# The first half of an adaLN modulation: sums moved to TensorE, and the first tile of x loaded ahead of the shift columns

## The chip, the core and the metric

The kernel runs on one core of a Trainium2 chip. The metric is device time in microseconds (us). Five engines matter: TensorE (PE in the rows, PEld its weight loads), VectorE (DVE), ScalarE (ACT), GpSimd (POOL), and SyncE (SP), which issues the transfers.

## What is computed

One layer of a decoder trunk over a sequence of 2048 tokens with 1024 columns, in float32. What the change touches is its first line:

```python
c_act = jax.nn.silu(c)                                        # 1024 values
shift, scale, gate = jnp.split(c_act @ w_ada + b_ada, 3, axis=-1)
h = rms_norm(x, norm_g) * (1 + scale[:, None]) + shift[:, None]
proj = h @ w_in                                               # 4232 columns
```

The projection feeds three mixers (a gated MLP, an mLSTM and a stick-breaking attention); their outputs go through one output projection, are multiplied by the gate and added to x.

## The kernel before

The 2048 tokens are 16 tiles of 128, taken in blocks of 5, 5 and 6 tiles. The first block is the prologue of this text. For its five tiles, x is loaded (`load_x`), ScalarE squares and sums it and GpSimd makes the scale of each row (`rms_x`), VectorE multiplies it by that scale and by `hscale`, VectorE or GpSimd adds `hshift` (`mod_x`: VectorE for tiles 0, 2 and 4, GpSimd for 1 and 3), TensorE transposes it, and ScalarE and VectorE write it as a high and a low part into `hT` (`hT_half`). Then TensorE multiplies it with the weights, which are split into two parts as well (`weights`), in three matmuls per 128 rows of weights (`proj_tc`, lines 297 to 299).

All of that is done in two halves of 512 columns: first columns 0 to 511 of all five tiles with the first half of the modulation, and the first four of eight row groups of the weights; then the other half. Of each half of the modulation, `ada` makes `hscale` (from the scale columns of w_ada) and `hshift` (from the shift columns). It sums over the 1024 rows of w_ada in eight groups of 128: six by VectorE, one multiply-add each into `acc`, which starts as a row of b_ada over zeros; two by TensorE into PSUM; and one matmul with a matrix of ones adds up `acc` over the partitions. So the sums stand in every partition. A float32 matmul is two instructions in the trace.

The transfers of w_ada come in four parts of 1 MiB for each half, scale columns first. All loads and stores of the rows below stand in one queue, SP's, in the order of the program. The tiles `x4va` and `x4gu` are the two halves of tile 4; `wad` is w_ada, `st` the staged weights, `wr` the split ones, `pada` the PSUM of the modulation, `pt` that of the transposes, `pc` that of the projection. The memory of `wad` and of the staged weights is used again for later loads, which wait until it is free. Two of the staged buffers exist, so the third set of weights needs the first to be split.

The order of the instructions on each engine is not the order of the code: a scheduler orders them with a modelled timeline, so an edit near the start can move instructions later too.

Of the kernel before, what the change touches and what calls it, by code (L numbers as in the profile page):

```python
# [18 lines left out]
P = 128  # L19
# [3 lines left out]
KT = D // P  # L23
# [10 lines left out]
def hybrid_block_kernel(ctx: ExitStack, tc: tile.TileContext, x, c, norm_g, w_ada, b_ada, w_in,  # L34
                        ga_v_norm, ga_ws, ga_bs, mb_conv_w, mb_conv_b, mb_b_i, mb_b_f, mb_h_norm,
                        sc_q_norm, sc_k_norm, w_out, out):
    nc = tc.nc
# [33 lines left out]
    c_act = const.tile([P, KT], F32, name="c_act")  # L71
# [36 lines left out]
    def flat(t):  # L108
        return t.rearrange("p a t -> p (a t)")

    def t512(name):
        return flat(tmp.tile([P, 4, P], F32, tag="t512", bufs=T5, name=name))
# [3 lines left out]
    def load_x(i, j, halves=None):  # L116
        if halves is None:
            if j % 4 < 2:
                xt = tmp.tile([P, D], F32, tag="xt", name=f"xt{i}")
            else:  # L120
                xt = stk.tile([P, D], F32, tag="aT", bufs=4, name=f"xt{i}")
            nc.sync.dma_start(xt, x[0, i * P:(i + 1) * P, :])
            xtiles[i] = [[xt], None]
        else:
            for hh in range(2):
                nc.sync.dma_start(halves[hh], x[0, i * P:(i + 1) * P, hh * 512:(hh + 1) * 512])
            xtiles[i] = [halves, None]

    def rms_x(i):
        parts = xtiles[i][0]  # L130
        ssq = tmp.tile([P, 2], F32, tag="ssq", bufs=6, name=f"ssq{i}")
        for n, xp in enumerate(parts):
            junk = tmp.tile([P, D], BF16, tag="t512", bufs=T5, name=f"junk{i}_{n}")
            nc.scalar.activation(junk[:, :xp.shape[1]], xp, AF.Square, accum_out=ssq[:, n:n + 1])
        s0 = ssq[:, 0:1]
        if len(parts) == 2:
            nc.gpsimd.tensor_tensor(s0, s0, ssq[:, 1:2], ALU.add)
        nc.gpsimd.tensor_scalar(s0, s0, 1.0 / D, EPS, ALU.mult, ALU.add)
        nc.gpsimd.tensor_tensor(s0, s0, neghalf[:, 0:1], ALU.pow)
        xtiles[i][1] = s0  # L140
# [11 lines left out]
    def vg_halves(i):  # L152
        return [tmp.tile([P, 2 * NBMAX * 64], F32, tag=tag, bufs=1, name=f"x{i}{tag}")[:, 0:512] for tag in ("va", "gu")]
# [11 lines left out]
    def load_w(src, segs, kp):  # L165
        st = stg_p.tile([P, 2, WMAX], F32, tag="st", name=f"st{ntag[0]}_{kp}")
        o = 0
        for c0, w in segs:
            nc.sync.dma_start(st[:, :, o:o + w],
                              src[kp * 256:(kp + 1) * 256, c0:c0 + w].rearrange("(a p) f -> p a f", p=P))  # L170
            o += w
        return st

    def weights(src, segs, kps=range(KT // 2), staged=None):

        W = sum(w for _, w in segs)
        tiles = []
        key = segs[0][0]
        made = split.setdefault(key, {})
        for kp in kps:  # L180
            if kp * 2 in made:
                for k in (2 * kp, 2 * kp + 1):
                    wt = wr_p.tile([P, 2, WMAX], F32R, tag="wr", name=f"wr{ntag[0]}_{k}")
                    nc.sync.dma_start(wt[:, :, :W].bitcast(F32), made[k])
                    tiles.append(wt)
                continue
            st = staged[kp] if staged else load_w(src, segs, kp)
            for a in range(2):
                wt = wr_p.tile([P, 2, WMAX], F32R, tag="wr", name=f"wr{ntag[0]}_{kp}_{a}")
                nc.scalar.copy(wt[:, 0, :W], st[:, a, :W])  # L190
                (nc.vector if a == 0 else nc.gpsimd).tensor_tensor(  # L191
                    wt[:, 1, :W], st[:, a, :W], wt[:, 0, :W].bitcast(F32), ALU.subtract)
                made[2 * kp + a] = dram.tile([P, 2, W], F32, name=f"w_d{key}_{2 * kp + a}")
                nc.sync.dma_start(made[2 * kp + a], wt[:, :, :W].bitcast(F32))
                tiles.append(wt)
        ntag[0] += 1
        return tiles

    def c_segs(p):
        segs = [(OFF["cq"] + p * P, P), (OFF["ck"] + p * P, P), (OFF["cv"] + p * P, P)]  # L200
        return segs + [(OFF["bi"], 8)] if p == 0 else segs
# [10 lines left out]
        nc.gpsimd.memset(brow[n], 0.0)  # L212
    g_bc = [stk.tile([P, 512], F32, tag="be", bufs=4, name=f"g_bc{n}") for n in range(2)]

    def ada_load(half):
        for n, c0 in enumerate((1024 + 512 * half, 512 * half)):
            for hh in range(2):
                nc.sync.dma_start(wad_buf[2 * n + hh], w_ada[0, 512 * hh:512 * hh + 512, c0:c0 + 512]
                                  .rearrange("(k p) f -> p k f", p=P))

    def ada(half):
        cs = slice(half * 512, half * 512 + 512)
        for n, c0 in enumerate((1024 + 512 * half, 512 * half)):
            pa = flat(pat.tile([P, 4, P], F32, tag="at", name=f"pada{half}_{n}"))
            acc = brow[c0 // 512]
            w0, w1 = wad_buf[2 * n], wad_buf[2 * n + 1]
            for k in range(6):
                nc.vector.scalar_tensor_tensor(acc, (w0 if k < 4 else w1)[:, k % 4, :], c_act[:, k:k + 1], acc,
                                               ALU.mult, ALU.add)
            for k in (6, 7):  # L230
                nc.tensor.matmul(pa, lhsT=c_act[:, k:k + 1].to_broadcast([P, P]), rhs=w1[:, k % 4, :],
                                 start=k == 6, stop=False)
            nc.tensor.matmul(pa, lhsT=ones_sq, rhs=acc, start=False, stop=True)
            if n == 0:
                nc.vector.scalar_tensor_tensor(hscale[:, cs], pa, 1.0, g_bc[half], ALU.add, ALU.mult)
            else:
                nc.scalar.copy(hshift[:, cs], pa)

    nc.sync.dma_start(crow, c.rearrange("o (k p) -> (o k) p", p=P))
    for n in (2, 0, 3, 1):  # L240
        nc.sync.dma_start(brow[n][0:1, :], b_ada[:, n * 512:(n + 1) * 512])
    ada_load(0)
    for n in range(2):
        nc.sync.dma_start(g_bc[n], norm_g[:, n * 512:(n + 1) * 512].broadcast_to([P, 512]))
    nc.gpsimd.dma_start(rows[R_CW:R_CW + 24, :], mb_conv_w.rearrange("o t (m p) -> (o t m) p", p=P))
    nc.gpsimd.dma_start(rows[R_CB:R_CB + 6, :], mb_conv_b.rearrange("o (m p) -> (o m) p", p=P))
    nc.gpsimd.dma_start(rows[R_BS:R_BS + 4, :], ga_bs.rearrange("o g p -> (o g) p"))
# [9 lines left out]

    NB0 = BLOCKS[0]
    staged = {}
    for j in range(NB0):  # L260
        halves = None
        if j == 4:
            halves = vg_halves(4)
        elif j == 5:
            halves = [t512(f"x5_{hh}") for hh in range(2)]
        load_x(j, j, halves)
        if j < 2:
            staged[j] = load_w(w_in[0], c_segs(0), j)
    ada(0)
    for j in range(NB0):  # L270
        rms_x(j)
        if j == 0:
            wt0 = weights(w_in[0], c_segs(0), range(0, 2), staged)
    ada_load(1)
    pr = pat.tile([P, 4, P], F32, tag="at", name="pr")
    nc.tensor.transpose(pr[:, 0, 0:36], rows, ident[0:36, 0:36])
# [524 lines left out]
    for j in range(NB0):  # L801
# [8 lines left out]
        ps0.append(ps)  # L810
        run(proj_tc(ps[:, :W0], wt0, j, W0, range(0, 4)))
    ada(1)
    wt0 += weights(w_in[0], c_segs(0), range(2, 4), staged)
    nc.sync.dma_start(vn_bc, ga_v_norm.rearrange("o g d -> o (g d)").broadcast_to([P, 256]))
# [24 lines left out]
    for b, nb in enumerate(BLOCKS):  # L839
# [30 lines left out]
        else:  # L870
# [4 lines left out]
            for m, _ in enumerate(chain(tail, islice(cp, lead * KT + 1))):  # L875
                j = m // KT - 1
# [205 lines left out]
```

## Time and profile before

| | |
|---|---|
| median of 3 runs | 1470.33 us (1470.11 to 1472.72) |
| the profiled execution, own time | 1471.23 us |
| its span, first to last instruction | 1469.2 us |
| TensorE busy | 1393.4 us (95%) |
| TensorE weight loads busy | 1298.2 us (88%) |
| VectorE busy | 1018.8 us (69%) |
| ScalarE busy | 676.5 us (46%) |
| GpSimd busy | 647.6 us (44%) |
| mean rate of the transfers | 159 GB/s, above 290 in the first twentieth of the span |

Busy time says how long an engine had an instruction under way. A matmul on TensorE can be pipelined, so a busy TensorE is not one at its peak: its clock has two levels, 1.2 and 2.4 GHz, which the profile shows as a granted clock of 0.5 and 1.0. The profile was taken from a single execution; its durations are those of that execution.

### The profile page before, as it was taken

Reading aid. Unit: us, or ns where it says so; the run is one execution under the profiler, and the core shown is the slowest. Engines: PE = TensorE matmul, PEld = TensorE weight load, DVE = VectorE, ACT = ScalarE, POOL = GpSimd, SP = SyncE. Lnnn points to the kernel's source line nnn. Section 1 sums busy time; section 2 is a strip of 40 time slices with the busy share of each in tenths; the row PEclk is TensorE's granted clock in tenths of the full one; section 3 lists DMA queues with packets and bytes.
Section 4 is the critical chain, followed back from the end, with each engine's and each line's share of the span. In section 5 each row is a group of like instructions: output and inputs, shape, how many; then the busy total and the mean of one; then the engine's idle time right before and its main releaser. Section 6 shows DMA issues by size and latency. Waiting matters only on the chain.

```text
span 1469.2 us, 24957 instructions
## 1 busy us (share of the span) xinstructions
PE 1393.4 (95%) x8468; PEld 1298.2 (88%) x8468; DVE 1018.8 (69%) x1778; ACT 676.5 (46%) x1656; POOL 647.6 (44%) x1140
## 2 busy tenths in 40 slices
PE   5999999898999999999999999999999978999998
PEld 3789999798999999988999899989999867888887
DVE  6797554676995666588799976778778788444543
ACT  3364454453554444346467655556455655111110
POOL 4473553743433432554343343434445337435442
PEclk8999999999999999999999999999999999999999
DMA  9866776666535533633433344303432435555541
GB/s 324 293 204 206 237 228 197 208 202 236 191 128 176 198 116 124 222 100 127 148 105 126 104 146 137 102 15 120 157 102 69 156 113 153 178 160 154 175 154 58
DMA packets 187103, 233.19 MB, mean 159 GB/s; under 512 B 22714, under 2 KB 160344, under 8 KB 186976
## 3 DMA queue, kind: packets, MB, share of 16 engines
q1 hardware_dynamic: 186752, 231.59, 48.5%
q8 instruction: 67, 1.10, 0.3%
q14 instruction: 60, 0.49, 0.1%
q0 software_dynamic: 224, 0.02, 0.0%
HBM read 159.24 MB, written 72.31 MB: 158 GB/s over the span
## 4 chain that ended last, share of the span: by engine, by line
PE 66%; DVE 15%; DMA 6%; issue 5%; POOL 4%; ACT 2%; SPq 1%; POOLq 0%; DVEq 0%; ACTq 0%
DVE bb L414 5%; PE av L444 5%; PE at L429 4%; PE pc L297 4%; PE pc L299 4%; PE pc L298 4%; PE po L995 4%; PE po L997 3%; PE po L996 3%; PE pg L297 3%; PE pg L298 3%; PE pg L299 3%; DMA st<-in_w_in_dram 2%; PE z L401 2%; PE z L402 2%
## 5 line engine op out<-in xcount | busy, mean ns | idle before, releaser
L414 DVE TENSOR_TENSOR_SCAN bb<-bb,bb 128x513 f32<-128x513 f32 x144 | 191.3, 1328 | 25.5 <-ACT bb L406 24.7
L418 POOL TENSOR_TENSOR be<-be,bb 128x512 f32<-128x512 f32 (+3 forms) x120 | 133.0, 1108 | 132.9 <-DVE bb L414 81.4
L432 DVE TENSOR_TENSOR aT<-at,aT 128x512 fp32r<-128x512 f32 (+3 forms) x240 | 142.3, 598 | 39.8 <-ACT aT L431 39.1
L406 ACT ACTIVATE bb<-z 128x512 f32<-128x512 f32 (+3 forms) x240 | 130.2, 543 | 80.5 <-PE z L402 61.2
L444 PE MATMUL av<-aT,Vst 128*128 128x256 f32 x816 | 148.7, 295 | 17.8 <-DVE aT L432 13.0
L431 ACT CAST aT<-at 128x512 fp32r<-128x512 f32 (+3 forms) x240 | 126.6, 529 | 83.8 <-PE at L429 82.7
L444 PEld LDWEIGHTS av<-aT,Vst 128*128 128x128 f32 x816 | 119.9, 189 | 30.1 <-DVE aT L432 21.0
L429 PE MATMUL at<-ident,be 128*128 128x128 f32 x816 | 132.7, 274 | 5.2 <-DVE aT L432 2.3
L297 PE MATMUL pc<-wr,hT 128*128 128x384 f32 (+1 forms) x384 | 134.8, 355 | 2.8 <-ACT hT L290 1.3
L299 PE MATMUL pc<-wr,hT 128*128 128x384 f32 (+1 forms) x384 | 134.7, 351 | 1.6 <-DVE hT L291 1.5
L298 PE MATMUL pc<-wr,hT 128*128 128x384 f32 (+1 forms) x384 | 133.4, 347 | 0.0
L407 ACT ACTIVATE be<-z 128x512 f32<-128x512 f32 (+3 forms) x240 | 131.7, 549 | 0.0
L429 PEld LDWEIGHTS at<-ident,be 128*128 128x128 f32 x816 | 99.2, 141 | 14.2 <-DVE aT L432 3.7
L995 PE MATMUL po<-wo,yT 128*128 128x512 f32 x256 | 104.9, 410 | 0.3 <-ACT yT L984 0.3
L414 DVE TENSOR_TENSOR_SCAN bb<-bb 128x129 f32<-128x129 f32 (+3 forms) x96 | 87.1, 911 | 23.3 <-POOL bb L409 16.8
L405 POOL MEMSET bb<- 128x1 f32 x240 | 23.5, 100 | 177.6 <-DVE bb L414 123.6
L996 PE MATMUL po<-wo,yT 128*128 128x512 f32 x256 | 101.6, 397 | 0.0
L997 PE MATMUL po<-wo,yT 128*128 128x512 f32 x256 | 101.4, 399 | 0.0
L487 PE MATMUL pb<-hT,wr 128*128 128x320 f32 (+1 forms) x288 | 93.2, 324 | 1.2 <-DMA wr<-w_d 1.2
L489 PE MATMUL pb<-hT,wr 128*128 128x320 f32 (+1 forms) x288 | 92.1, 323 | 1.8 <-DVE wr L191 1.3
L297 PE MATMUL pa<-wr,hT 128*128 128x384 f32 x256 | 88.2, 347 | 5.1 <-DVE qk L360 2.4
L401 PE MATMUL z<-Kst,Qst 128*128 128x512 f32 (+3 forms) x240 | 90.2, 385 | 2.4 <-DVE Kst L371 1.6
(273 smaller groups left out, 3900.3 us busy)
## 6 DMA issues: line engine op xcount, KB each, us to landing
wr<-w_d SPq DMA_DIRECT2D x160, 384.0 KB, 5.6
w_d<-wr SPq DMA_DIRECT2D x80, 384.0 KB, 3.4
wad<-in_w_ada_dram SPq DMA_DIRECT2D x8, 1024.0 KB, 6.7
xo<-in_x_dram SPq DMA_DIRECT2D x16, 512.0 KB, 3.8
out_dram<-o SPq DMA_DIRECT2D x31, 256.0 KB, 2.9
xt<-in_x_dram SPq DMA_DIRECT2D x15, 512.0 KB, 4.9
st<-in_w_in_dram SPq DMA_DIRECT2D x60, 128.0 KB, 3.4
wr<-w_d SPq DMA_DIRECT2D x16, 392.0 KB, 6.2
```

The costliest lines, as they stand in the source:

```text
L297: nc.tensor.matmul(ps, lhsT=hT[:, 0, k, cols], rhs=wt[k][:, 0, :W], start=k == 0, stop=False)
L298: nc.tensor.matmul(ps, lhsT=hT[:, 0, k, cols], rhs=wt[k][:, 1, :W], start=False, stop=False)
L299: nc.tensor.matmul(ps, lhsT=hT[:, 1, k, cols], rhs=wt[k][:, 0, :W], start=False, stop=k == KT - 1)
L407: nc.scalar.activation(be[:, :w], z[:, :w], AF.Sigmoid)
L414: nc.vector.tensor_tensor_scan(rev, rev, rev, carry.get((i, h), 1.0), ALU.mult, ALU.bypass)
L418: eng.tensor_tensor(be[:, :w], be[:, :w], bb[:, 1:w + 1], ALU.mult)
L429: nc.tensor.transpose(at[:, s, :], be[:, s * P:(s + 1) * P], ident)
L432: nc.vector.tensor_tensor(aT[:, :nb_, 1, :], at[:, :nb_, :], aT[:, :nb_, 0, :].bitcast(F32), ALU.subtract)
L444: nc.tensor.matmul(flat(av), lhsT=Vst[:, s0 + s, h, :], rhs=flat(aT[:, s]), start=(s0 + s == i), stop=(s0 + s == 0))
L995: nc.tensor.matmul(po, lhsT=yT[:, 0, k, :], rhs=wo[k][:, 0, cs], start=k == 0, stop=False)
L996: nc.tensor.matmul(po, lhsT=yT[:, 0, k, :], rhs=wo[k][:, 1, cs], start=False, stop=False)
L997: nc.tensor.matmul(po, lhsT=yT[:, 1, k, :], rhs=wo[k][:, 0, cs], start=False, stop=k == KT - 1)
```

## The change

Two edits. In the first half of the modulation all eight groups of rows are summed by TensorE (`nv = 0`), so VectorE's twelve multiply-adds of that half go and twelve matmuls come; the second half stays as it was. And the loads are put in another order: the scale columns of w_ada, x tile 0, the first half of norm_g, then the shift columns; the second half of norm_g goes behind all x tiles. The squares of tile 0 are written ahead of the others.

```diff
-    def ada_load(half):
-        for n, c0 in enumerate((1024 + 512 * half, 512 * half)):
+    def ada_load(half, ns=range(2)):
+        for n in ns:
+            c0 = 512 * half + (1024 if n == 0 else 0)
...
-            for k in range(6):
+            nv = 6 if half else 0
+            for k in range(nv):
                 nc.vector.scalar_tensor_tensor(acc, (w0 if k < 4 else w1)[:, k % 4, :], c_act[:, k:k + 1], acc,
                                                ALU.mult, ALU.add)
-            for k in (6, 7):
-                nc.tensor.matmul(pa, lhsT=c_act[:, k:k + 1].to_broadcast([P, P]), rhs=w1[:, k % 4, :],
-                                 start=k == 6, stop=False)
+            for k in range(nv, KT):
+                nc.tensor.matmul(pa, lhsT=c_act[:, k:k + 1].to_broadcast([P, P]), rhs=(w0 if k < 4 else w1)[:, k % 4, :],
+                                 start=k == nv, stop=False)
             nc.tensor.matmul(pa, lhsT=ones_sq, rhs=acc, start=False, stop=True)
...
-    ada_load(0)
-    for n in range(2):
-        nc.sync.dma_start(g_bc[n], norm_g[:, n * 512:(n + 1) * 512].broadcast_to([P, 512]))
+    ada_load(0, [0])
+    load_x(0, 0)
+    nc.sync.dma_start(g_bc[0], norm_g[:, 0:512].broadcast_to([P, 512]))
+    ada_load(0, [1])
...
+    rms_x(0)
     for j in range(NB0):
...
-        load_x(j, j, halves)
+        if j > 0:
+            load_x(j, j, halves)
...
     ada(0)
-    for j in range(NB0):
+    wt0 = weights(w_in[0], c_segs(0), range(0, 2), staged)
+    for j in range(1, NB0):
         rms_x(j)
-        if j == 0:
-            wt0 = weights(w_in[0], c_segs(0), range(0, 2), staged)
+    nc.sync.dma_start(g_bc[1], norm_g[:, 512:1024].broadcast_to([P, 512]))
     ada_load(1)
```

ScalarE, from the first square to the first cast of transposed x; before. `junk` is the square of a tile (168, 175, 182, 184 and x4va are tiles 0 to 4), `wr` the split weights, and line 237 the copy of the shift.

```order
L134 ACTIVATE junk_0_213,ssq_212<-xt_168 128x1024
L237 COPY hshift<-pada_1_201 128x512
L190 CAST wr_0_0_217<-st_0_170 128x392
L190 CAST wr_0_1_222<-st_0_170 128x392
L134 ACTIVATE junk_0_238,ssq_237<-xt_175 128x1024
L190 CAST wr_1_0_227<-st_1_177 128x392
L190 CAST wr_1_1_232<-st_1_177 128x392
L290 CAST hT<-pt_0_280 128x4x128
```

The same place with the change; the tiles 0 to 4 are xt_152, 179, 186, 188 and x4va, and the copy of the shift is line 239.

```order
L134 ACTIVATE junk_0_170,ssq_169<-xt_152 128x1024
L190 CAST wr_0_0_216<-st_0_174 128x392
L190 CAST wr_0_1_221<-st_0_174 128x392
L134 ACTIVATE junk_0_237,ssq_236<-xt_179 128x1024
L190 CAST wr_1_0_226<-st_1_181 128x392
L190 CAST wr_1_1_231<-st_1_181 128x392
L134 ACTIVATE junk_0_242,ssq_241<-xt_186 128x1024
L134 ACTIVATE junk_0_247,ssq_246<-xt_188 128x1024
L134 ACTIVATE junk_0_252,ssq_251<-x4va 128x512
L239 COPY hshift<-pada_1_205 128x512
L134 ACTIVATE junk_1_254,ssq_251<-x4gu 128x512
L295 CAST hT<-pt_0_280 128x4x128
```

The copy of the shift has moved from behind the first square to behind the square of half of tile 4.

VectorE, at the second half of the modulation; before. `brow_136` is the sum for the shift, line 235 makes the scale, line 149 multiplies and line 150 adds.

```order
L235 SCALAR_TENSOR_TENSOR hscale<-pada_0_388,g_bc_144 128x512
L228 SCALAR_TENSOR_TENSOR brow_136<-wad_132,c_act,brow_136 128x512
L149 SCALAR_TENSOR_TENSOR xt_168<-xt_168,ssq_212,hscale 128x512
L149 SCALAR_TENSOR_TENSOR xt_175<-xt_175,ssq_237,hscale 128x512
L149 SCALAR_TENSOR_TENSOR xt_182<-xt_182,ssq_242,hscale 128x512
L149 SCALAR_TENSOR_TENSOR xt_184<-xt_184,ssq_247,hscale 128x512
L149 SCALAR_TENSOR_TENSOR x4gu<-x4gu,ssq_252,hscale 128x512
L191 TENSOR_TENSOR wr_2_0_410<-st_2_268,wr_2_0_410 128x392
L150 TENSOR_TENSOR xt_168<-xt_168,hshift 128x512
```

The same place with the change (the sum is line 230, the scale line 237).

```order
L237 SCALAR_TENSOR_TENSOR hscale<-pada_0_388,g_bc_144 128x512
L149 SCALAR_TENSOR_TENSOR xt_152<-xt_152,ssq_169,hscale 128x512
L149 SCALAR_TENSOR_TENSOR xt_179<-xt_179,ssq_236,hscale 128x512
L149 SCALAR_TENSOR_TENSOR xt_186<-xt_186,ssq_241,hscale 128x512
L149 SCALAR_TENSOR_TENSOR xt_188<-xt_188,ssq_246,hscale 128x512
L149 SCALAR_TENSOR_TENSOR x4gu<-x4gu,ssq_251,hscale 128x512
L230 SCALAR_TENSOR_TENSOR brow_136<-wad_132,c_act,brow_136 128x512
L191 TENSOR_TENSOR wr_3_0_420<-st_3_273,wr_3_0_420 128x392
L829 COPY wsT<-pw 128x512
L230 SCALAR_TENSOR_TENSOR brow_136<-wad_132,c_act,brow_136 128x512
L191 TENSOR_TENSOR wr_0_0_665<-st_0_663,wr_0_0_665 128x384
L150 TENSOR_TENSOR xt_152<-xt_152,hshift 128x512
```

The last two sums for the shift now stand behind the five multiplies, the last one behind a weight split and the copy of `wsT` too; a split of the next stage's weights stands ahead of the first add.

## Rows read from the trace of the kernel before

**Rows 1.** Busy us by stretch (and instructions), granted TensorE clock, DMA share, GB/s.

```profile
0.00:23.19 23.19, 8.42 (x14) 3.12 (x15) 12.87 (x20) 5.89 (x11) 9.75 (x27) 0.94 0.94 324
23.19:31.00 7.81, 6.94 (x23) 5.57 (x24) 5.32 (x9) 4.38 (x11) 6.68 (x10) 0.51 1.02 365
31.00:34.00 3.00, 1.51 (x8) 0.69 (x5) 2.56 (x4) 0.80 (x2) 1.65 (x2) 1.00 0.98 333
34.00:38.00 4.00, 3.91 (x15) 3.81 (x16) 3.31 (x6) 0.00 (x0) 0.00 (x0) 0.57 0.72 262
38.00:51.00 13.00, 12.24 (x56) 9.04 (x54) 11.71 (x18) 3.27 (x7) 1.12 (x3) 1.00 0.68 229
51.00:60.00 9.00, 6.13 (x27) 5.16 (x28) 4.62 (x10) 3.02 (x7) 7.82 (x6) 0.81 0.69 225
60.00:120.00 60.00, 56.22 (x378) 54.28 (x378) 51.37 (x100) 35.97 (x99) 34.54 (x69) 1.00 0.74 252
```

**Rows 2.** Timeline, first half: start, us, engine, line, operation [idle before <-releaser].

```profile
6.55 4.69 DVE L228 SCALAR_TENSOR_TENSOR brow<-wad,c_act,brow 128x512 f32<-128x512 f32 x6 [3.58 <-DMA wad<-in_w_ada_dram]
...
9.54 3.75 PE L231 MATMUL pada<-wad,c_act 128*128 128x512 f32 x4 [6.98 <-DMA wad<-in_w_ada_dram]
...
15.14 1.98 PE L231 MATMUL pada<-wad,c_act 128*128 128x512 f32 x4 [0.71 <-DMA wad<-in_w_ada_dram]
...
18.35 1.06 ACT L134 ACTIVATE junk<-xt 128x1024 bf16<-128x1024 f32 x1 [15.57 <-DMA xt<-in_x_dram]
...
19.40 0.57 ACT L237 COPY hshift<-pada 128x512 f32<-128x512 f32 x1
...
23.22 1.09 PE L289 MATMUL pt<-ident,xt 128*128 128x128 f32 x4 [4.11 <-ACT wr L190]
...
26.91 0.62 ACT L134 ACTIVATE junk<-x4va 128x512 bf16<-128x512 f32 x1
```

**Rows 3.** Chain of waits, 34 to 48 us: start, us from instruction to instruction.

```profile
35.69 0.33 PE pc L297
...
39.92 0.44 PE pt L289 x4
40.36 0.18 PE pc L297
...
42.51 1.72 PE pada L231 x4
...
44.58 0.87 PE pada L233 x2
```

**Rows 4.** Timeline, second half of the modulation, several engines.

```profile
45.44 0.94 ACT L190 CAST wr<-st 128x392 fp32r<-128x392 f32 x2 [4.46 <-DMA st<-in_w_in_dram]
...
46.74 2.73 DVE L149 SCALAR_TENSOR_TENSOR xt<-xt,ssq,hscale 128x512 f32<-128x512 f32 x4
...
47.07 1.88 PE L231 MATMUL pada<-wad,c_act 128*128 128x512 f32 x4
...
49.84 0.58 ACT L237 COPY hshift<-pada 128x512 f32<-128x512 f32 x1 [3.46 <-PE pada L233]
...
50.07 3.72 POOL L191 TENSOR_TENSOR wr<-st,wr 128x392 fp32r<-128x392 f32 x1
...
52.82 0.68 DVE L824 COPY wsT<-pw 128x512 f32<-128x512 f32 x1
...
53.74 2.50 POOL L150 TENSOR_TENSOR xt<-xt,hshift 128x512 f32<-128x512 f32 x2
...
55.06 1.11 PE L289 MATMUL pt<-ident,xt 128*128 128x128 f32 x4 [1.84 <-POOL xt L150]
...
57.59 0.93 ACT L190 CAST wr<-st 128x384 fp32r<-128x384 f32 x2 [5.04 <-DMA st<-in_w_in_dram]
...
58.60 1.01 POOL L191 TENSOR_TENSOR wr<-st,wr 128x384 fp32r<-128x384 f32 x1 [0.79 <-ACT wr L190]
```

## The prediction

> **What bounds the kernel now.** I read the busy times by stretch first, then the engines' timelines of the first 60 us, then the chain that ended last. Over the whole span TensorE is busy 1393.4 of 1469.2 us, so the time is TensorE's instructions plus 76 us in which it has none. The change touches only work done before about 55 us: after some 600 of TensorE's 8,100 instructions the order of both programs is the same on every engine. So the question is how many of TensorE's idle or half-clock microseconds near the start go or come. By stretch [rows 1], TensorE is idle 14.8 us before its first transposes at 23.2 us, 2.45 us from there to 38 us (0.87, 1.49 and 0.09), 3.6 us from 51 to 60 us (the second half of the modulation comes late) and 3.8 us from 60 to 120 us. Its granted clock is 0.51 in 23.2 to 31 us and 0.57 in 34 to 38 us, which means mostly the 1.2 GHz level; a projection matmul then starts every 0.33 us, against 0.18 us at 2.4 GHz [rows 3].
>
> The first modulation in the kernel before [rows 2]: the quarters of w_ada land at 6.55 (VectorE begins), 9.54 and, the last, about 15.1 us. The first x tile lands at 18.35 us, the shift's copy starts at 19.40 us and the transposes at 23.22 us. That is the chain to beat.
>
> **Part 1: TensorE sums alone.** It removes 12 VectorE multiply-adds of 0.78 us (the first six took 4.69 us [rows 2]). They were hidden: VectorE has 10 us of slack before 23 us [rows 1], and only the last one held up the shift. It adds 12 matmuls, each two instructions like those of L231. Four such instructions take 1.72 us at 2.4 GHz [rows 3], so 0.43 each, and the four from 9.54 us take 3.75 us, about 0.85 apart [rows 2], which is the 1.2 GHz pitch; the granted clock of 0.94 up to 23.19 us [rows 1] does not show this, so I go by the pitch. With the closing sums TensorE has 36 instructions of this size. They start at 6.55 us. In the kernel before the pitch was down to half by 15.14 us after work since 9.54; I take about 4.2 us at the slow pitch (5 instructions), then 31 at 0.43: the shift's sum is ready at 6.55 + 4.2 + 13.3 = 24.1 us. The data is there sooner: with 3.0 us per 1 MiB quarter (6.55 to 9.54), and x tile 0 (1.5 us) and one half of norm_g (0.75 us) now ahead of them, the shift quarters land at 14.8 and 17.8 us. So the shift's sum comes some 5 us later than before, when its copy began at 19.40 us.
>
> **Part 2: x ahead, and where the shift's copy stands.** Tile 0 lands at about 11.0 us instead of 18.35; its square and its scale are finished long before they are wanted. But the order on ScalarE puts the copy of the shift behind the squares of tiles 1, 2, 3 and half of tile 4. Bytes ahead of that half tile are fewer by one half of norm_g, so it lands about 0.75 us earlier than the queue of before would give, at about 25.3 us; in the kernel before its square ran at 26.91 us [rows 2]. So the copy runs from about 26.3 to 26.9 us whatever TensorE does, up to 2 us of lateness in the sum being covered. Queued behind the copy are the casts of the transposed tiles. VectorE has the scale of tile 3 (ready after its square and power, about 27.4 us) ahead of the add of tile 0, so that add ends at 28.1 us and the transposes start there: **+4.9 us** against 23.2.
>
> **Part 3: the first half of the projection.** At 2.4 GHz it is 60 matmuls at 0.18, five groups of transposes at 0.44, two pairs of sums at 1.72 and one closing pair at 0.87 [rows 3]: 17.3 us. Before, it ran from 23.2 to 48.8 us (the last pair of sums starts at 47.07 [rows 4], plus 1.72), 25.6 us: 17.3, 2.45 idle, and the rest, 5.9 us, is the 1.2 GHz level in its two stretches. After, every x tile has landed and been scaled when the stream starts, so I expect one slow stretch. From the rows of before it may cost 1.5 to 3.7 us (the stretches lasted some 3.4 and 7.4 us, half of which is loss); I take 3.0, since this start has the same gaps between transposes, cast and first matmul as the longer one. Idle I take as 1.0 (0.6 to 2.5). So 28.1 + 21.3 = 49.4 us: **-4.3 us**, together +0.6.
>
> **Part 4: the second modulation.** The half of norm_g that it needs is now behind the x tiles, but lands by about 27 us and is wanted at 45: free. The last quarter of w_ada has moved in SP's queue behind the third staged weights and the four stores of split weights. Exactly the bytes that stood ahead of the end of those weights before stand ahead of it now, and those landed at 45.4 us [rows 4]. So two VectorE sums (k = 4, 5) come after 45.4 us. VectorE now has, from TensorE's sum of the scale at about 45.5 us: the scale and five multiplies at 0.68, a sum at 0.78, a weight split and the copy of wsT at 0.68 (the split at most), and, behind these, the last sum at 0.78 [rows 2, 4]: 7.0 us, to 52.5. TensorE's closing pair takes 0.87 [rows 3], the shift's copy 0.58 [rows 4]: 53.9 us, against 50.4 before. Queued behind the last sum on VectorE are its own adds; the transposes wait for them. What follows is better, though: before, GpSimd took 3.72 us over a split that takes 1.01 alone, since VectorE ran two-input adds beside it, and its add of tile 1 started only at 53.74 us [rows 4]; now two splits are done before the shift. Tile 1's add (1.25 us, half of 2.50) ends at 55.1 us alone, at 57 if VectorE's three adds go first; I take 55.7. Before, the transposes of tile 1 started at 55.06 us [rows 4], 6.3 us after the last pair of sums; now 6.3 us too: **0**. Two matmuls that ran before 55 us then do not now: **+0.4 us** (0.33 to 0.7).
>
> By the Trainium skill's page "SBUF — State Buffer" (section "Who interferes with whom"), a VectorE instruction with two SBUF inputs keeps a GpSimd instruction that reads SBUF out for its whole length. The 3.72 us split agrees [rows 4]. By that rule the five multiplies would hold up the next split as well, which is the second rival below.
>
> **Part 5: after 60 us.** Three weight splits of the next stage move ahead of the transposes, off the time when VectorE is most loaded (51.4 of 60 us busy from 60 to 120 us [rows 1]). Nothing shows this price. The bounds are all of TensorE's 3.8 idle us there gone, and 2 us more idle from the changed order; I take **-0.5**, nearer to nothing, since most waits there belong to the scans.
>
> **Sum.** +4.9 - 4.3 + 0 + 0.4 - 0.5 = +0.5 us on the profiled execution's 1471.2 us (span 1469.2 and 2.0 around it), which stands 0.9 us above the median of the runs, 1470.33. On that median: **1470.8 us**, no change. What a measurement tells from no change is 0.2%, 2.9 us.
>
> **Rivals.** (1) *The stage after 60 us gains.* If the earlier splits take away all of the 3.8 us that TensorE waits from 60 to 120 us, instead of 0.5, and the slow stretch of part 3 is the short one (1.5 less), the time is 1470.8 - 3.3 - 1.5 = 1466.0 us. For it: VectorE is the loaded engine there. Against: the scans there, which fill most of it, are not changed, and the shift of part 4 is late. Chance 0.27, faster.
>
> (2) *The second shift comes late because GpSimd is kept out.* If the five multiplies (3.4 us) keep out GpSimd's split of the third staged weights as the adds did before, it ends at about 49 us instead of 46, and the load of the next stage's first weights, which waits for that buffer, goes out 3 us later. Such a load landed 3.8 us after the split before (53.79 to 57.59 [rows 4]), so at 52.8 us; two casts (0.93 [rows 4]) and a split that must wait for VectorE's adds to end at about 56 us stand ahead of the add of tile 1 on GpSimd. That add then ends at 56 + 1.0 + 1.25 = 58.3 us instead of 55.7, with TensorE idle: +2.6, and a longer slow stretch after the longer gap up to 1 more: 1470.8 + 3.5 = 1474.3 us. It decides if the add of tile 1 ends after 58 us. For it: the 3.72 us split. Against: a split may start before the multiplies do. Chance 0.20, slower.
>
> (3) *TensorE's sum stays at 1.2 GHz.* Then 36 instructions at 0.85 end at 37.2 us, the copy waits for TensorE and not for x, and the transposes start at about 38.5 us, 10 us later: 1481 us. For it: the slow pitch from 9.54 us on. Against: that pitch was gone by 15.14 us with less work done. The Trainium skill's page "TensorE: Matmul & The Clock Gate" (section "What's actually happening") has the slow level as the state after idling, released by sustained work; by that rule this rival falls. Chance 0.06, slower.
>
> **How the numbers follow.** No change 0.47, rival 1 0.27, rivals 2 and 3 0.26 together. The range reaches to rivals 1 and 2 and a microsecond past the second, 1466.0 to 1475.5 us, and leaves rival 3 and the far ends of the bounds out. The likeliest case's own range is 1468 to 1473 us.
>
> **What would show it.** Right: the first transposes at 27 to 29 us, with ScalarE's copy of the shift right behind the square of half of tile 4; no idle over 1 us on TensorE from there to the last pair of sums at about 48 us; the second shift's copy at 53 to 54 us. Wrong: a first copy that waits for TensorE (then the clock decides, rival 3), first transposes before 25 us, or tile 1's second transposes over 2 us away from 55.7 us; and if TensorE's idle time from 60 to 120 us changes by over 2 us, part 5 was the one that mattered.

## The result and the profile after

The changed kernel took 1481.76 us (median of 6 runs, 1476.84 to 1482.16) against 1472.59 us (1470.11 to 1475.28) for the kernel before, run beside it: a ratio of 1.0055 with a 95% interval of 1.0039 to 1.0071. In a second measurement it took 1484.06 us against 1474.77, 1.0070 (1.0057 to 1.0083). It is 9 us slower; the forecast was no change, with a range that ended at 1475.5 us.

The busy times by stretch of the profile after come first (span 1477.0 us; columns as in [rows 1]).

```profile
0.00:23.19 23.19, 16.77 (x36) 7.58 (x37) 3.01 (x7) 5.63 (x10) 9.16 (x26) 1.00 0.93 314
23.19:31.00 7.81, 2.53 (x11) 1.71 (x9) 6.63 (x8) 4.48 (x10) 6.35 (x9) 0.74 1.00 312
31.00:34.00 3.00, 3.00 (x11) 2.49 (x10) 2.86 (x5) 0.70 (x2) 0.79 (x3) 0.55 0.91 344
34.00:38.00 4.00, 4.00 (x27) 3.88 (x26) 3.93 (x7) 0.72 (x2) 0.00 (x0) 1.00 1.05 395
38.00:51.00 13.00, 11.45 (x54) 8.71 (x52) 10.97 (x16) 2.97 (x7) 2.52 (x3) 1.00 0.97 326
51.00:60.00 9.00, 3.94 (x12) 2.26 (x12) 8.08 (x10) 3.55 (x7) 7.25 (x6) 0.68 0.94 300
60.00:120.00 60.00, 55.83 (x354) 53.28 (x354) 47.13 (x91) 31.51 (x89) 31.71 (x65) 0.96 0.59 196
```

Against [rows 1], TensorE has 4.4 us less work from 23.2 to 31 us and 1.5 us more from 31 to 34 us, there at a granted clock of 0.55. From 34 to 38 us it is busy throughout, as before, but at a granted clock of 1.00 where it was 0.57, and gets 27 instructions done instead of 15. Then comes the hole from 51 to 60 us: 3.94 us busy where it was 6.13. From 60 to 120 us its idle time is 4.2 us, before 3.8.

The timeline of the first half, which answers to [rows 2]:

```profile
6.66 8.66 PE L233 MATMUL pada<-wad,c_act 128*128 128x512 f32 x16 [4.12 <-DMA wad<-in_w_ada_dram]
...
22.88 1.02 PE L235 MATMUL pada<-brow,ones_sq 128*128 128x512 f32 x2
...
29.37 1.97 PE L294 MATMUL pt<-ident,xt 128*128 128x128 f32 x8 [5.28 <-DVE xt L150]
...
25.65 0.61 ACT L134 ACTIVATE junk<-x4va 128x512 bf16<-128x512 f32 x1
...
26.27 0.56 ACT L239 COPY hshift<-pada 128x512 f32<-128x512 f32 x1
...
26.95 1.76 DVE L149 SCALAR_TENSOR_TENSOR xt<-xt,ssq,hscale 128x512 f32<-128x512 f32 x1 [0.42 <-POOL ssq L139]
28.64 2.36 DVE L150 TENSOR_TENSOR xt<-xt,hshift 128x512 f32<-128x512 f32 x2
...
26.90 1.26 POOL L150 TENSOR_TENSOR xt<-xt,hshift 128x512 f32<-128x512 f32 x1
```

The sums were ready at 23.9 us and the copy of the shift waited for nothing but the square ahead of it, as forecast. The transposes came 6.15 us later than before, 1.3 us more than forecast. VectorE's add of tile 0, which they wait for, took 0.68 us; late was the multiply of tile 3 ahead of it, 1.76 us (0.75 for those of tiles 0 and 2) beside GpSimd's add of tile 1, which had begun 0.05 us earlier.

The second half of the modulation, which answers to [rows 4], in the timelines of TensorE, VectorE, ScalarE and GpSimd:

```profile
47.13 1.88 PE L233 MATMUL pada<-wad,c_act 128*128 128x512 f32 x4
...
52.85 1.13 PE L235 MATMUL pada<-brow,ones_sq 128*128 128x512 f32 x2 [3.40 <-DVE brow L230]
55.47 2.16 PE L294 MATMUL pt<-ident,xt 128*128 128x128 f32 x8 [1.49 <-DVE xt L150]
57.28 0.68 PE L302 MATMUL pc<-wr,hT 128*128 128x392 f32 x1
57.75 0.53 PE L303 MATMUL pc<-wr,hT 128*128 128x392 f32 x1
60.61 0.69 PE L304 MATMUL pc<-wr,hT 128*128 128x392 f32 x1 [2.33 <-DVE hT L296]
...
45.91 3.07 DVE L149 SCALAR_TENSOR_TENSOR xt<-xt,ssq,hscale 128x512 f32<-128x512 f32 x4
...
49.56 1.50 DVE L230 SCALAR_TENSOR_TENSOR brow<-wad,c_act,brow 128x512 f32<-128x512 f32 x1
...
52.06 0.74 DVE L230 SCALAR_TENSOR_TENSOR brow<-wad,c_act,brow 128x512 f32<-128x512 f32 x1
...
54.63 2.38 DVE L150 TENSOR_TENSOR xt<-xt,hshift 128x512 f32<-128x512 f32 x2 [0.92 <-ACT hshift L239]
56.93 1.76 DVE L150 TENSOR_TENSOR x4gu<-x4gu,hshift 128x512 f32<-128x512 f32 x1
58.61 1.34 DVE L191 TENSOR_TENSOR wr<-st,wr 128x384 fp32r<-128x384 f32 x1
59.87 1.28 DVE L296 TENSOR_TENSOR hT<-pt,hT 128x512 fp32r<-128x512 f32 x2
...
54.01 0.58 ACT L239 COPY hshift<-pada 128x512 f32<-128x512 f32 x1 [2.14 <-PE pada L235]
...
45.41 1.03 POOL L191 TENSOR_TENSOR wr<-st,wr 128x392 fp32r<-128x392 f32 x1
49.11 1.40 POOL L191 TENSOR_TENSOR wr<-st,wr 128x392 fp32r<-128x392 f32 x1 [2.68 <-ACT wr L190]
...
54.67 3.46 POOL L150 TENSOR_TENSOR xt<-xt,hshift 128x512 f32<-128x512 f32 x2
```

The same adds, and the first low part of `hT` behind them, in VectorE's timeline before, and below them the start of TensorE's steady stream before:

```profile
50.53 1.28 DVE L150 TENSOR_TENSOR xt<-xt,hshift 128x512 f32<-128x512 f32 x2
51.74 0.68 DVE L150 TENSOR_TENSOR x4gu<-x4gu,hshift 128x512 f32<-128x512 f32 x1
...
53.42 0.68 DVE L291 TENSOR_TENSOR hT<-pt,hT 128x512 fp32r<-128x512 f32 x1
...
55.83 0.68 PE L299 MATMUL pc<-wr,hT 128*128 128x392 f32 x1
```

Up to the last pair of sums the kernels are level: 47.13 us against 47.07. Then TensorE waits for VectorE's last sum (3.40), for its first add (1.49) and for the low part of `hT` (2.33). The shift's copy is 4.2 us late; the adds take 4.1 us instead of 1.9, since GpSimd's two adds (3.46) now run beside them; and the split ahead of the low parts takes 1.34 us beside one of GpSimd's (a split and the copy of `wsT` stood there before, 0.56 and 0.68). The steady projection starts at 60.61 us instead of 55.83, 4.8 us late. Compared instruction by instruction, TensorE is 4.9 us behind at 155 us; the order of the instructions differs up to about 147 us and is that of before from there.

Why the sums are late is in SP's timeline, here the loads of w_ada for the second half; before:

```profile
23.03 0.46 SPq L218 DMA_DIRECT2D wad<-in_w_ada_dram  x1
...
28.06 0.41 SPq L218 DMA_DIRECT2D wad<-in_w_ada_dram  x1
```

And after:

```profile
30.82 0.38 SPq L219 DMA_DIRECT2D wad<-in_w_ada_dram  x1
...
38.11 0.37 SPq L219 DMA_DIRECT2D wad<-in_w_ada_dram  x1
```

These are the shift's two quarters. The second of them has landed at 46.6 us in the trace, at 40.0 us before, and the two sums that need it stand behind the multiplies. SP's order has the loads behind stores and staged weights. Their buffers are those of the first shift, which TensorE's sum now holds until 23 us (VectorE's last sum ended at 17.7 us before); but the loads go out 8 and 15 us after that. What they waited for is SP's queue: the stores and staged weights ahead of them, and, the first of them, 2.4 us for an earlier load of w_ada to land. That the longer hold is why the scheduler put them there is argued and not shown.

### The profile page after: what moved, and what is told of

It reads as the page before. It is cut to its first block, busy times and chain, and to the rows that moved or that the text cites. A ratio compares the mean times of both kernels' runs of the same rounds, so it can differ in the third digit from the quotient of the medians.

```text
span 1477.0 us, 24988 instructions
## 1 busy us (share of the span) xinstructions
PE 1400.9 (95%) x8492; PEld 1300.2 (88%) x8492; DVE 1015.2 (69%) x1766; ACT 678.6 (46%) x1656; POOL 641.6 (43%) x1140
## 4 chain that ended last, share of the span: by engine, by line
PE 64%; DVE 15%; DMA 8%; POOL 5%; issue 5%; ACT 2%; SPq 1%; POOLq 0%; DVEq 0%; ACTq 0%
DVE bb L419 5%; PE av L449 5%; PE at L434 4%; PE pc L302 4%; PE pc L304 3%; PE pc L303 3%; PE po L1001 3%; PE po L1002 3%; PE pg L302 3%; PE pg L303 3%; PE po L1000 3%; PE pg L304 3%; DMA wad<-in_w_ada_dram 2%; DMA st<-in_w_in_dram 2%; PE z L406 2%
```

## The experiments

The table compares each kernel's profile with the first profile of before, TensorE instruction by instruction: how far it is behind at about 155 us (late), and what is added between 374 and 439 us. Then the medians beside the kernel before on the same chip.

| kernel | late | 374 to 439 | median | before | ratio (95%) |
|---|---|---|---|---|---|
| after | 4.9 | 2.9 | 1481.76 | 1472.59 | 1.0055 (1.0039 to 1.0071) |
| after, again | 5.7 | 4.3 | 1484.06 | 1474.77 | 1.0070 (1.0057 to 1.0083) |
| e1, sums alone | 4.7 | 2.2 | 1482.63 | 1475.56 | 1.0042 (1.0027 to 1.0057) |
| e2, loads alone | 6.3 | 0.3 | 1481.48 | 1475.56 | 1.0039 (1.0024 to 1.0054) |
| e3, adds on VectorE | 5.7 | 2.9 | 1482.64 | 1475.56 | 1.0050 (1.0036 to 1.0064) |
| e8, four sums | 3.5 | 3.1 | 1480.64 | 1475.56 | 1.0037 (1.0023 to 1.0052) |
| e7, before, 1 MiB more | 9.9 | 0.1 | 1482.33 | 1473.93 | 1.0050 (1.0033 to 1.0068) |
| e9, three edits | 3.3 | 5.8 | 1483.62 | 1473.93 | 1.0058 (1.0042 to 1.0075) |
| e12, before, adds on VectorE | 3.6 | 0.4 | 1480.01 | 1473.93 | 1.0038 (1.0025 to 1.0051) |
| e15, after, two sums out | 0.5 | 2.6 | 1478.05 | 1474.77 | 1.0022 (1.0013 to 1.0032) |
| e18, before, two sums out | -0.4 | -0.1 | 1475.29 | 1474.77 | 1.0012 (1.0000 to 1.0025) |
| e17, before, half a MiB more | 3.6 | 0.1 | 1477.65 | 1474.77 | 1.0027 (1.0018 to 1.0037) |
| e20, before, 12 matmuls more | -1.1 | 1.8 | 1475.96 | 1472.34 | 1.0025 (1.0015 to 1.0034) |
| e21, after, 20 matmuls more | 9.1 | 0.7 | 1479.80 | 1472.34 | 1.0055 (1.0037 to 1.0073) |
| e22, after, 36 matmuls more | 13.2 | 0.6 | 1489.86 | 1472.34 | 1.0125 (1.0109 to 1.0142) |

**e1 and e2, one edit each.** e1 is the kernel before with the first edit, e2 the changed kernel without it:

```diff
-            for k in range(6):
+            nv = 6 if half else 0
+            for k in range(nv):
...
-            for k in (6, 7):
+            for k in range(nv, KT):
```

```diff
-            nv = 6 if half else 0
+            nv = 6
```

> The sums edit alone; the loads stand as in the kernel before. Its order of the second modulation is that of the changed kernel (last two sums for the shift behind five multiplies, a split and the copy of wsT; two splits of the next stage ahead of the first low part of hT). Theory 1 (the loss is made in the second modulation, from 47 to 61 us, by that order): as slow as the changed kernel, 1479 to 1482 us, second shift copied near 54 us, second stream of matmuls from 60 to 61 us. Theory 2 (the loss comes from the loads: the shift columns behind x tile 0, the last quarter of w_ada behind the stores): near the kernel before, 1471 to 1475 us.

> The order of loads alone; VectorE keeps its six sums per half. Its order of the second modulation has the last two sums together ahead of all splits, and one split ahead of the first low part of hT. Theory 1: most of the loss goes, 1472 to 1477 us, second shift copied at 50 to 52 us, second stream from 56 to 58.5 us. Theory 2: as slow as the changed kernel, 1479 to 1482 us.

The sums alone bring the same order and the same loss: the closing pair at 52.11 us behind VectorE's sum, the stream at 58.65 (forecast for 60 to 61). The loads alone lose as much by another wait, which neither theory had:

```profile
52.09 2.08 PE L235 MATMUL pada<-brow,ones_sq 128*128 128x512 f32 x2 [3.57 <-DVE brow L230]
...
59.61 1.09 PE L294 MATMUL pt<-ident,xt 128*128 128x128 f32 x4 [2.92 <-DVE wsT L829]
```

Here too the last sum is behind the multiplies, and the transposes of tile 1 wait for the copy of `wsT`, which frees their PSUM. Each edit alone makes the second shift late; they don't add up.

**e3, all adds of the second half on VectorE** (edit of the change).

```diff
-        mod_x(j, hh * 512, hh * 512 + 512, nc.vector if j % 2 == 0 else None)
+        mod_x(j, hh * 512, hh * 512 + 512, nc.vector if hh or j % 2 == 0 else None)
```

> The changed kernel, with VectorE making all five adds of the second half (GpSimd made those of tiles 1 and 3). Theory 1, as far as the two engines hold each other up: the adds take 0.6 us each again (three took 4.1 us in the changed kernel), so five end at about 57.7 instead of 58.7 us, and the second stream starts 1 to 2 us earlier: 1 to 2.5 us less than the changed kernel. Theory 2, or if the adds do not hold each other up: no gain, or up to 1 us more, for VectorE has two adds more.

No gain: the closing pair still waits 3.23 us, and the five adds of one engine take 3.9 us (55.06 to 58.97), as long as three beside GpSimd's two (4.1). So taking the adds off GpSimd gives nothing back; that says that the mutual slowing is not by itself what costs.

**e8, the second shift's sums four by VectorE, four by TensorE** (edit of the change).

```diff
-            nv = 6 if half else 0
+            nv = (6, 4)[n] if half else 0
```

> The changed kernel, with groups 4 to 7 of the second shift's sum on TensorE (6 and 7 before), so that VectorE's last sums are those of k = 0 to 3 and come before the multiplies. Theory 1: TensorE's wait of 3.4 us ahead of the closing pair goes, less 1.7 us for the four more instructions; second shift copied at about 52 us instead of 54.0; the stream starts 2 us earlier or more, as one split also moves behind: 2 to 4 us less than the changed kernel. Theory 2: no gain, 0 to 2 us more for the added matmuls.

The transposes come at 53.70 and 54.83 us and the stream at 57.66, still behind a low part of `hT`. 1.4 us of the lateness is gone, and the medians are too near to tell more.

**Before once more.**

> The kernel before once more, for a second profile of it. If late waits differ from execution to execution, its TensorE instructions after 160 us stand up to 3 us off those of the first profile although the first 160 us agree within 0.5 us; if they do not, all stand within 0.5 us to the end, and what the variants lose after 160 us is theirs.

It took 1473.97 us. Its first 270 us agree with the first profile within 0.5 us; later it is up to 3.3 us behind, 2.8 at the end. So a difference of 3 us after 270 us in one pair of profiles is no finding by itself.

**e7 and e17, a late start alone.** Part of w_ada is loaded once more ahead of everything in the kernel before, 1 MiB in e7 (all 512 columns), half of that in e17.

```diff
+    nc.sync.dma_start(wad_buf[0][:, :, 0:256], w_ada[0, 0:512, 0:256].rearrange("(k p) f -> p k f", p=P))
     ada_load(0)
```

> The kernel before with 1 MiB of w_ada loaded once more ahead of everything (into a buffer that is then overwritten), so that the whole prologue starts some 3 us later and nothing else is meant to change. If lateness in the prologue is passed on one to one to the end: 2 to 4 us slower than before. If it is absorbed by later waits: within 1 us. If lateness draws more lateness behind it: 5 us or more.

> The kernel before with half a MiB of w_ada loaded once more ahead of everything; the order of the instructions on all engines is that of the kernel before. By 3.0 us a MiB the first quarter lands 1.5 us later. Theory, the loss of the changed kernel comes with the order of its second modulation: here only the lateness shows, at most 2 us at 150 us, and the time is 1473 to 1476 us. Rival, a late start grows by itself, as 3 us became 10 when a whole MiB stood ahead: 4 us or more at 150 us, 1478 us or more.

In e7 the order of the second modulation changed too, and the second transposes came at 61.11 us, after 8.41 us without work; so it is no test of lateness alone. In e17, with the order of before, the first transposes are 3.1 us late (the load cost twice what I took, so the time lies above the 1473 to 1476 us of the theory), and it is 3.6 us at 155 us: lateness alone is handed on nearly as it is. Its median is 2.9 us behind.

**e9 and e12, attempts to win.** e9 has the edits of e3 and e8 and the loading and copy of `wsT` moved behind the second half; e12 is the kernel before with the edit of e3.

> The changed kernel with three edits together: groups 4 to 7 of the second shift on TensorE, all five adds of the second half on VectorE, and the transposition of the gMLP weights (wsl, wsT) behind the second half. Theory 1 (loss made in the second modulation): the stream starts at 56 to 57 us instead of 60.6 and the time is 1 to 3 us above the kernel before, or less. If the loss after e3 and e8 sits elsewhere: 5 us above the kernel before, as e8.

> The kernel before, with VectorE making all five adds of the second half. Theory 1: the transposes of tile 1 no longer wait for GpSimd's 3.72 us split and its add (they started at 55.06), so the stream starts at 53 to 54 us and the time is 1 to 3 us under the kernel before. If the adds on VectorE cost as much as they free, as in e3: no difference beyond 1 us.

Both miss. e9 starts its stream at 57.50 us but loses 5.8 us from 374 to 439 us. e12 has the transposes of tile 1 at 53.53 us, earlier than before, and then waits for the casts of `hT` (1.27 and 2.27 us).

**e15 and e18, the two late sums left out**, in the changed kernel and in the one before (there `range((6, 4)[n] if half else 6)`).

```diff
-            for k in range(nv):
+            for k in range((6, 4)[n] if half else 0):
```

> The changed kernel without VectorE's sums k = 4 and 5 of the second shift (left out of the computation: two of eight row groups of the shift columns, half of the columns). Theory, the late sums hold the second shift's copy and with it the low parts of hT: the copy comes at 50 to 51 us, the stream at 56 to 57.5 us, at 150 us at most 1.5 us behind the first profile of before, and the time is 1473 to 1476 us. Rival, the other order of the stage from 60 to 160 us is what costs: the copy is early all the same, but 4 us or more are lost by 150 us, and the time is 1479 us or more.

> The kernel before without the same two sums (left out of the computation as in the kernel above), whose order from 60 to 160 us changes too. Theory of the late sums: in the kernel before they were done long before the shift's copy at 49.8 us, so nothing is gained or lost: 1471 to 1475 us. Rival, any other order of the stage from 60 to 160 us costs: 1478 us or more.

TensorE's timeline in e15:

```profile
49.78 1.02 PE L235 MATMUL pada<-brow,ones_sq 128*128 128x512 f32 x2
...
52.62 0.66 PE L294 MATMUL pt<-ident,xt 128*128 128x128 f32 x4 [1.38 <-DVE xt L150]
53.75 0.66 PE L294 MATMUL pt<-ident,xt 128*128 128x128 f32 x4 [0.47 <-POOL xt L150]
...
57.49 0.70 PE L304 MATMUL pc<-wr,hT 128*128 128x392 f32 x1 [1.79 <-DVE hT L296]
```

The lateness falls from 4.9 and 5.7 us to 0.5, and 6 us of the median go; in the kernel before the same cut changes 0.5 us, at the edge of its interval. So the two sums are what makes the prologue late. But e15 still loses 3.3 us in the median with 0.5 us of lateness, 2 us more than its theory allowed. That remainder has a second cause.

**Again the change, and e20 to e22: what happens near 415 us.**

> The changed kernel once more. If the loss sits in the start, the profile shows the same start: last pair of sums at 47 us, the second copy of the shift at 54 us, TensorE's stream at 60.6 us, 4.5 to 5.5 us behind the first profile of the kernel before at 150 us; the median 1480 to 1483 us. If the stretch up to 150 us is as uneven from run to run as what follows, these instants move by 2 us or more.

The start is some 1 us later than in the first profile (lateness and median just above what was expected) and the loss from 374 to 439 us larger. By the table, the seven profiles with the first half's sums on TensorE, and no further matmuls added, lose 2.2 to 5.8 us there; those with these sums on VectorE, e20 aside, at most 0.4. SP issues three loads of split weights at that place. One of them took 1.92 us in the first profile after, 1.29 in the second and 0.57 before, and in that microsecond (413 to 414) the queue that the page calls instruction moved a packet:

```profile
q8 instruction: 1, 0.02, 9.4%
```

Such 16 KB packets come about one per 260 TensorE instructions here, and the change adds 48 (24 matmuls with their weight loads). e20 adds 48 to the kernel before, e21 80 and e22 144 to the changed one:

```diff
+    for _ in range(12):
+        nc.tensor.matmul(pcr[:, 1, 0:8], lhsT=ident, rhs=ident[:, 0:8], start=True, stop=True)
```

> The kernel before with twelve matmuls of 8 columns (48 instructions on TensorE, as many as the change adds there) behind the transposes of c, while TensorE waits for w_ada; the order of everything else is that of the kernel before. Theory: loads of instructions go in packets of 16 KB, one per some 256 TensorE instructions; with 48 more, one falls on SP's issue of split weights near 409 us, as in all seven profiles with the sums on TensorE. Then one of the three issues there takes 1.2 us or more instead of 0.57, TensorE loses 2 to 4 us between 374 and 439 us, the first 150 us are those of before within 0.5 us, and the time is 1476 to 1479 us. Rival: that loss comes from the late start or by chance; then the issues take 0.57 each, under 1 us is lost there, and the time is 1473 to 1475.5 us.

> The changed kernel with twenty such matmuls (80 instructions) at the same place, the order of some rows before 150 us changes with them. Theory: the packet moves away from SP's issue at 413 us by some 6 us or more; the issues take 0.57 each and under 1 us is lost from 374 to 439 us, where the changed kernel lost 2.9 and 4.3; the time is 1478 to 1481 us. Rival: 2 us or more are lost there all the same, 1481 to 1485 us.

> The same with 36 matmuls (144 instructions). Theory: the packets fall nearly where they fall in the kernel before; the issues near 413 us take 0.57 each, under 1 us is lost from 374 to 439 us, and the time is 1478 to 1481 us. Rival: 2 us or more are lost there all the same, 1481 to 1485 us.

The same three issues and TensorE's wait behind them, first before (its second profile):

```profile
409.54 1.90 SPq L184 DMA_DIRECT2D wr<-w_d  x3
...
414.87 0.41 PE L487 MATMUL pb<-hT,wr 128*128 128x320 f32 x1 [0.78 <-DMA wr<-w_d]
```

The changed kernel:

```profile
413.30 3.25 SPq L184 DMA_DIRECT2D wr<-w_d  x3
...
418.38 0.42 PE L492 MATMUL pb<-hT,wr 128*128 128x320 f32 x1 [1.03 <-DMA wr<-w_d]
420.82 0.41 PE L492 MATMUL pb<-hT,wr 128*128 128x320 f32 x1 [1.73 <-DMA wr<-w_d]
```

e20, the kernel before with 48 more TensorE instructions:

```profile
409.35 2.45 SPq L184 DMA_DIRECT2D wr<-w_d  x3
...
415.27 0.41 PE L489 MATMUL pb<-hT,wr 128*128 128x320 f32 x1 [1.02 <-DMA wr<-w_d]
```

e21, and below it e22:

```profile
416.30 1.90 SPq L184 DMA_DIRECT2D wr<-w_d  x3
```

```profile
422.29 1.90 SPq L184 DMA_DIRECT2D wr<-w_d  x3
```

e20's packet fell at 409.8 us, inside the issues, and behind as many TensorE instructions (4518) as in the changed kernel (4513). It was 1.1 us ahead of before at 155 us and lost 1.8 us from 374 to 439 us (the theory had 2 to 4, with one issue above 1.2 us; the three took 0.55 more than before in all). Its profile ended 5.1 us behind the first of before and 2.4 behind the second; the median, 1475.96 us, is 3.6 us behind and lies between the ranges of the theory and the rival. In e21 and e22 the packet came 4.4 and 11 us ahead of the issues, all three took 1.90, and 0.6 to 0.7 us is lost. e21 is 3.4 us later at 155 us than the changed kernel was in its later profile, by another order; its median loses 7.5 us, where the changed kernel lost 9.2 and 9.3, but with four runs the intervals overlap. e22's median is 4 us above what its lateness gives, above both ranges; its profile does not show why.

Not all of the loss in this stretch lies at the issues. In e20 0.7 us is lost at 381 to 384 us, 0.6 near 393 and 0.5 behind the issues; in the changed kernel 0.6, 0.5 and 1.7. The middle step is there without such a packet too: the second profile of before has 0.3 there, e21 and e22 0.5. The first follows the packet before (369.9 us in e20), which fell while a load of the gate columns of w_ada was under way. VectorE, in e20 and below it before:

```profile
373.04 0.75 DVE L741 SCALAR_TENSOR_TENSOR gacc<-stgate,c_act,gacc 128x512 f32<-128x512 f32 x1 [1.33 <-DMA stgate<-in_w_ada_dram]
```

```profile
371.98 0.75 DVE L739 SCALAR_TENSOR_TENSOR gacc<-stgate,c_act,gacc 128x512 f32<-128x512 f32 x1
```

Nor is this the only such meeting, and the kernel before has its own. Over all 17 profiles, SP's issues of split weights took 0.56 us in the median and over 0.9 us in 87 of 2863 cases (3%) where no packet moved during them, and over 0.9 us in 60 of the 129 where one did. Of these long ones the kernels whose packet falls at the issues near 415 us have four or five each, all others two or three.

## Why the prediction was wrong

**What held.** Part 1: the shift's sum was forecast for 24.1 us and was ready at 23.9; rival 3 (the slow level all along) fell, since the second 16 instructions took 7.03 us, 0.43 each. Part 2: the copy was forecast behind the square of x4va at 26.3 us and began at 26.27; only the transposes were 1.3 us later than the 28.1 forecast, by VectorE's multiply beside GpSimd's add. Part 3: the stream gave that back and more, 6.1 us where I had 4.3, with one slow stretch from 31 to 34 us; I had 0.6 us of net lateness at the last pair of sums, 0.06 came. That this is so near is luck in part, since the errors of parts 2 and 3, 1.3 and 1.8 us, cancel. The stage from 60 to 120 us gained nothing, against rival 1.

**The step that failed is the end of part 4**, "Two matmuls that ran before 55 us then do not now: +0.4 us". The wait before it was sized well: the second shift's copy was forecast to end at 53.9 us and ended at 54.6, and tile 1's transposes, forecast for 55.7, are the second four of the eight that run from 55.47 to 57.63 us, under a microsecond late. I took the stream to start with them. But its third matmul needs the low part of `hT`, which VectorE writes only after its own three adds and a split, and both sides of that are in the profile: adds beside GpSimd's last 4.1 us instead of 1.9, and the split 1.34 instead of 0.56. The term is 4.9 to 5.7 us, not 0.4. I had counted the adds' slowing as something that the new order takes away, since the split that it had held up before (3.72 us [rows 4]) was now done sooner; it came back between the adds. e15 shows the cause ahead of it: without the two late sums the lateness is 0.5 us. My signs of being wrong stood on the wrong instruction, too: tile 1's transposes came within 0.8 us of 55.7 and the idle time from 60 to 120 us changed by 0.4 us, so none of them told of the loss.

**Rival 2 had the place and not the mechanism.** The five multiplies did not keep GpSimd's split of the third staged weights out: it began at 45.41 us, 0.5 us ahead of them, took its 1.03 us, and it was the first multiply that waited (1.08 us, the next ones 0.74). The next split, at 49.11 us, met only the last of the multiplies and took 1.40 us. GpSimd's add of tile 1 ended at 56.45 us, not after 58, and was not what the stream waited for.

**What no part had** is the remaining 3 to 4 us. I wrote that the change "touches only work done before about 55 us". That was wrong twice. The order of the instructions differs up to about 147 us; this cost the changed kernel nothing, since its lateness is 4.8 us at the start of the stream and 4.9 at 155 us. And behind that the order is the same, but the place of the instruction packets in it is not. Over the eight profiles whose packet meets the issues near 415 us (the seven and e20), the loss of the median is above the lateness by 3.4 us in the mean (1.4 to 6.4). Over the other seven variants it is above it by 0.5 us in the mean (-1.6 to 4.3, the top being e22, then e12 with 2.5), so the two groups overlap. e20 shows that 48 more instructions on TensorE are enough to cost the median 3.6 us, with an order of the rest that is that of before. Shown is that an issue that meets a packet often takes longer, and that one load under way beside a packet landed late. That these meetings make up the whole of the remaining 3 to 4 us is not shown, and why the packets moved by about 100 instructions of the program and not by 48 stays open.

No version beat the kernel before.

## What to carry to other kernels

When a sum moves to another engine, look first at what becomes of the next load into its input buffer: here it went out later, and the sums that need it were put behind everything that was ready sooner. Follow the late result past the first instruction that uses it, to the last operand of the steady stream (here the low part behind the adds, not the transposes). And before trusting a small loss or gain far from an edit, add the same number of idle instructions to the kernel before: if that alone moves the time, what the edit does at its own place need not be what did it.

## What the runs showed of the hardware

Where a 16 KB packet of the instruction queue moved during one of SP's issues of split weights, 60 of 129 issues took over 0.9 us, 3% of the others; near 415 us it was 1.29 to 1.92 us instead of 0.57 in the changed kernel. The Trainium skill's page "Runtime: NRT & Kernel Launch" (section "Instruction fetch mechanics") has instructions refilled in blocks of 16 KiB, 256 instructions, and calls the cost mostly hidden. The size agrees with the packets here (252 to 264 TensorE instructions apart from 374 to 419 us in the two profiles compared); the cost was not hidden where a packet met an issue.

VectorE and GpSimd, each with two inputs in SBUF, kept each other out in turn, whichever had begun. Of VectorE's three adds in the second half the first took 0.69 us, the next two 1.77 and 1.76 (0.68 each before); GpSimd's two beside them took 1.78 and 1.72 (1.27 and 1.28 before). Why the 3.72 us split before had to wait for several of VectorE's instructions on end, where these adds took turns, is not shown.

A window of the granted clock that lies ahead of the first entry of the trace's clock record reads 1.00. In the profile after, this record begins at 9.80 us. The matmuls from 6.66 us on start 0.85 to 0.99 us apart until then and 0.43 us apart from 10.0 us on, so the pitch shows the slow level, 1.2 GHz, which the 1.00 of the first 23 us does not.
